# Gate steps one per unit over the experts' first products, residual products among the index picks, and another split of the weights' low parts between VectorE and GpSimd

## The chip, the cores and the metric

The program runs on one core of a Trainium2 chip. The metric is the device time of one execution in microseconds; the time of a kernel is the median over its runs.

## What is computed

The reference is two transformer blocks on 256 tokens of width 1024. The change lies in the second block's feed-forward part, which picks experts for each token:

```
q = (xc @ w_query).reshape(T, 8, 2, 128)
s1, s2 = q[:, :, 0] . sub_keys_1, q[:, :, 1] . sub_keys_2      # 128 scores per head and half
v1, i1 = top_k(s1, 16); v2, i2 = top_k(s2, 16)                 # first choice
cand   = v1[..., :, None] + v2[..., None, :]                   # 256 candidates
best, pos = top_k(cand, 16)                                    # second choice
idx = take_along_axis(i1 * 128 + i2, pos); g = softmax(best)
act = gelu(xc . expert_u[idx]); out = sum(g * act * expert_v[idx])
x = rms_norm(x + out, final_norm_g)
```

## The kernel before

Nothing is gathered: all 16384 experts are computed densely, and a gate matrix, zero where a token did not choose an expert, weights them. An expert is a pair (i, j) of sub-key numbers; one weight tile of 128 experts (one j, all i) is a unit, so there are 128 units of first products (`eu`) and 128 of second products (`ev`). They run in two halves of 64: stage A (first products of units 0 to 63, with choice and gates woven in), its second products, stage B (first products of 64 to 127, with their gates), its second products.

Products in full fp32 precision are made of fp32r halves. Each weight tile of 512 KB is loaded by SP into `raw`; ScalarE (ACT) copies it into `hi`, and VectorE (DVE) or GpSimd (POOL) makes `lo` = `raw` - `hi`; a letter per tile (`v` or `g` in `BY2` for the block's weights, `BYU` for `eu`) says which. TensorE (PE) then makes 24 products per unit, 16 with `hi` and the last 8 with `lo`. Tiles are fetched two units ahead (`ahead`), with three buffers each of `raw`, `hi` and `lo`.

Every engine works its queue in the order of the program's text, which is made by `weave`: after unit i of the first products (`experts_u`), `counts[i]` steps of a side generator are written. The lists are `CA` for stage A and `CB` for stage B. The side of stage A is `gen_a`:

- `second()`: eight steps with two heads of the second choice (`top16`, DVE alone), one that takes the positions apart, one softmax step, four index picks (one per token half t and key half i: a one-hot compare `eq`, a product with `ixr`, a tree of sums into `sel`, all on DVE), and two that transpose `sel` on PE and write `IT`, `JT`, `GHL`: 16 steps.
- `gates3()`: 33 steps, each for 8 tokens. A step makes the one-hots `oi`, `eqj` and `jg` of its tokens on DVE, and then PE makes the 16 products (line 1784) of the step before it, which ACT copies into the gates `Gt`. The last step only has products.

Stage B's side, `gen_b`, is the 33 gate steps alone. Behind its steps each generator calls `prep(0)`, which makes the first tiles of the second products: `act` times `Gt` on DVE (line 1811), `eh` on ACT, `el` on DVE. The gelu of the last two units is written when `experts_u` ends.

Ahead of stage A lies the query stage: 16 tiles of `w_query`, two per head, and the first choice of each head (`first`, `top16`) on DVE, which lags behind PE. `acc`, the four PSUM banks of the output, begins with the residual: 16 products of `xT` with the identity (line 1803; fp32, so 32 in the trace), written between the query stage and stage A.

In `CA` before, the second choice lies after units 14 to 21, positions and softmax after 24 and 25, the picks after 26, 28, 30 and 32, the transposes after 34 and 35; the gate steps run from unit 36 to 63, one per unit, but two after units 40, 45, 50, 55 and 60. In `CB` there is a gate step after every second unit from 2 to 58 and after each from 59 to 62; the entry at 63 writes `prep(0)`.

Of the kernel before, what the change touches and what calls it, by code (L numbers as in the profile page):

```python
# [13 lines left out]
AF = mybir.ActivationFunctionType  # L14
# [81 lines left out]
OUTS = (4, 6, 5, 7, 2, 3, 0, 1)  # L96
JOBS = ('hf', 'gq', 'hq', 'gk', 'gv', 'lqk', 'v5', 'v2', 'sm', 'hg', 'lg', 'z', 'fq', 'fk')
LAG = (1, 1)
CA = [0] * 14 + [1] * 8 + [0, 0, 1, 1] + [1, 0] * 4 + [1, 1] + [1, 1, 1, 1, 2] * 6
BYU = "g" * 26 + "v" * 38 + "g" * 64  # L100
CB = [0] * 2 + [1, 0] * 28 + [1] * 6

ND1 = 8
WARM = 8
# [2 lines left out]
BY1 = "v" * 37  # L107
TURNS1 = '0000000030000003030300030030010001333103030030303003300300303043004304555400510341011401000414141041000414124010142010412412420120121020112002122002002020000000000'
TURNS2 = '00000000000000000010000000100000101011011020010000100100110011212012021000202010020000020000020022022000002002020000000000000200000200000000000'
BY2 = 'vgvvvvvvgvgggvvgvgvvvvvggggvgggggggggvggvvgvvvgvgggvgvvvvgvggvvvgvg'  # L110
FU = "v"
FD = "v"

# [3 lines left out]
def _emit(ctx, tc, I, out):  # L117
    nc = tc.nc
    ctx.enter_context(tc.manual_schedule())
    V, S, G, PE = nc.vector, nc.scalar, nc.gpsimd, nc.tensor  # L120
# [20 lines left out]
    def A(o, i, f, **kw):  # L141
        t = tables.get(f)
        if t and t != table[0]:
            S.preload_act_table_set(t)
            table[0] = t
        S.activation(o, i, f, **kw)  # L146
# [6 lines left out]
    def plan(*items, by="v"):  # L153
        order.extend((n, i, w, by) for n, i, w in items)
# [40 lines left out]
    ident, mask = kept[:, 0:128], kept[:, 128:384]  # L195
    xT = keep.tile([128, 8, 256], F32)
# [13 lines left out]
    one_t = keep.tile([128, 1], F32)  # L210
# [247 lines left out]
    for lo_, hi_ in ((0, JA), (JA, 128)):  # L458
        for i in range(lo_, hi_):
            plan(("eu", i, 1024), by=BYU[i])  # L460
        plan(*[("ev", i, 1024) for i in range(lo_, hi_)])
# [769 lines left out]
    with tc.tile_pool(name="ffn", bufs=2) as fp:  # L1231
# [29 lines left out]
        acc = [bank() for _ in range(4)]  # L1261
# [399 lines left out]
    def second():  # L1661
        best = ktmp.tile([128, 2, 8, 16], F32, tag="best", name="best", bufs=1)
        pos = ktmp.tile([128, 2, 8, 16], U32, tag="pos", name="pos", bufs=1)
        for t in range(2):
            cd = ktmp.tile([128, 8, 112], F32, tag="cd", name="cd", bufs=1)
            v1, v2 = kv[:, t, 0], kv[:, t, 1]
            V.tensor_tensor(cd[:, :, 0:64].rearrange("p h (a b) -> p h a b", a=4),
                            v1[:, :, 0:4, None].to_broadcast([128, 8, 4, 16]),
                            v2[:, :, None, :].to_broadcast([128, 8, 4, 16]), op=OP.add)
            V.tensor_tensor(cd[:, :, 64:112].rearrange("p h (a b) -> p h a b", a=12),  # L1670
                            v1[:, :, 4:16, None].to_broadcast([128, 8, 12, 4]),
                            v2[:, :, None, 0:4].to_broadcast([128, 8, 12, 4]), op=OP.add)
            for h in range(0, 8, 2):
                top16(112, *((cd[:, i], best[:, t, i], pos[:, t, i]) for i in (h, h + 1)))
                yield

        ab = ktmp.tile([128, 4, 256], U32, tag="ab", name="ab", bufs=1)
        pf_ = pos.rearrange("p t h k -> p (t h k)")
        ge = ktmp.tile([128, 256], U32, tag="ge", name="ge", bufs=1)
        V.tensor_scalar(ab[:, 0], pf_, 4, None, op0=OP.logical_shift_right)  # L1680
        V.tensor_scalar(ab[:, 1], pf_, 15, None, op0=OP.bitwise_and)
        V.tensor_scalar(ab[:, 2], pf_, 2, None, op0=OP.logical_shift_right)
        V.tensor_scalar(ab[:, 3], pf_, 3, None, op0=OP.bitwise_and)
        V.tensor_scalar(ge, pf_, 6, None, op0=OP.logical_shift_right)
        abf = ktmp.tile([128, 4, 256], F32, tag="abf", name="abf", bufs=1)
        V.tensor_copy(abf, ab)
        V.tensor_scalar(abf[:, 2], abf[:, 2], 12.0, None, op0=OP.subtract)
        for i in range(2):
            V.copy_predicated(abf[:, i], ge, abf[:, 2 + i])
        abh = ktmp.tile([128, 2, 2, 8, 16], F16, tag="abh", name="abh", bufs=1)  # L1690
        V.tensor_copy(abh.rearrange("p i t h k -> p i (t h k)"), abf[:, 0:2])
        yield

        sel = ktmp.tile([128, 3, 2, 128], F32, tag="sel", name="sel", bufs=1)
        gg = sel[:, 2].rearrange("p t (h k) -> p (t h) k", h=8)
        bb = best.rearrange("p t h k -> p (t h) k")
        V.tensor_tensor(gg, bb, bb[:, :, 0:1].to_broadcast([128, 16, 16]), op=OP.subtract)
        A(gg, gg, AF.Exp)
        sm_ = ktmp.tile([128, 16], F32, tag="smk", name="smk", bufs=1)
        V.tensor_reduce(out=sm_, in_=gg, op=OP.add, axis=AX.X)  # L1700
        V.reciprocal(sm_, sm_)
        V.tensor_tensor(gg, gg, sm_[:, :, None].to_broadcast([128, 16, 16]), op=OP.mult)
        yield
        for t in range(2):
            for i in range(2):
                ixr = ktmp.tile([128, 8, 16, 16], F16, tag="ixr", name="ixr", bufs=2)
                A(ixr, kix[:, t, i, :, :, None].to_broadcast([128, 8, 16, 16]), AF.Copy)
                eq = ktmp.tile([128, 8, 16, 16], F16, tag="eq", name="eq", bufs=2)
                V.tensor_tensor(eq, abh[:, i, t, :, None, :].to_broadcast([128, 8, 16, 16]),
                                io16[:, None].to_broadcast([128, 8, 16, 16]), op=OP.is_equal)  # L1710
                V.tensor_mul(eq, eq, ixr)
                for w in (8, 4, 2):
                    V.tensor_add(eq[:, :, 0:w], eq[:, :, 0:w], eq[:, :, w:2 * w])
                V.tensor_add(sel[:, i, t].rearrange("p (h k) -> p h k", h=8), eq[:, :, 0], eq[:, :, 1])
                yield
        for t in range(2):
            p = bank("g")
            for i in range(3):
                PE.transpose(p[:, i * 128:i * 128 + 128], sel[:, i, t], ident)
            ts = slice(t * 128, t * 128 + 128)  # L1720
            two = lambda z: z[:, :, None].to_broadcast([128, 128, 2])
            V.tensor_copy(IT[:, ts], two(p[:, 0:128]))
            V.tensor_copy(JT[:, ts], two(p[:, 128:256]))
            gs = ktmp.tile([128, 128], F32, tag="gs", name="gs", bufs=1)
            V.tensor_scalar(gs, p[:, 256:384], 4096.0, None, op0=OP.mult)
            V.tensor_copy(GHL[:, ts, 0], two(gs))
            V.tensor_sub(GHL[:, ts, 1], two(gs), GHL[:, ts, 0])
            yield
# [69 lines left out]
        prep(0)  # L1798

    acc = [bank() for _ in range(4)]  # L1800
    for t in range(2):
        for k in range(8):
            PE.matmul(acc[2 * t + k // 4][:, (k % 4) * 128:(k % 4) * 128 + 128], xT[:, k, t * 128:t * 128 + 128], ident,
                      start=k % 4 == 0, stop=False, skip_group_check=True)

    W = {}
# [9 lines left out]

    def experts_v(j0, nj, last):
        for j in range(0, nj, 2):
            if j + 2 < nj:
                prep(j + 2)  # L1820
            eh, el = W.pop(j)

            def rows(i, t, v, ns=(0, 1)):
                ts = slice(t * 128, t * 128 + 128)
                for n in ns:
                    o = acc[2 * t + n]
                    n_ = slice(n * 512, n * 512 + 512)
                    PE.matmul(o, eh[:, i, ts], v[0][:, n_], start=False, stop=False, skip_group_check=True)  # L1828
                    PE.matmul(o, el[:, i, ts], v[0][:, n_], start=False, stop=False, skip_group_check=True)  # L1829
                    PE.matmul(o, eh[:, i, ts], v[1][:, n_], start=False, stop=last and j + i == nj - 1,  # L1830
                              skip_group_check=True)

            if last and j + 2 == nj:
                vs = [weight("ev", j0 + j + i) for i in range(2)]
                for t in range(2):
                    for n in range(2):
                        for i in range(2):
                            rows(i, t, vs[i], (n,))
            else:
                for i in range(2):  # L1840
                    v = weight("ev", j0 + j + i)
                    for t in range(2):
                        rows(i, t, v)
                    ahead()
            yield

    weave(experts_u(0, JA), gen_a(), CA)
    run(experts_v(0, JA, False))
    weave(experts_u(JA, 128 - JA), gen_b(), CB)
    fg = xT[:, 0:4].rearrange("p a b -> p (a b)")  # L1850
    nc.sync.dma_start(fg, I["fng"].broadcast_to([128, 1024]))
    A(one_t, one_t, AF.Ln)
    run(experts_v(JA, 128 - JA, True))


    wx.close()
    last = ctx.enter_context(tc.tile_pool(name="last", bufs=2))
# [153 lines left out]
```

## Time and profile before

| | us |
|---|---|
| time before, median of 3 runs | 1512.96 (1509.63 to 1517.84) |
| the profiled execution's own time | 1508.16 |
| its span in the trace | 1506.4 |
| PE busy in the span | 1433.6 |
| DVE, ACT, POOL busy | 995.0, 779.8, 307.6 |

Busy times add the lengths of instructions of an engine, overlaps once; a weight load of PE lies beside its products. A wait is the idle time of an engine ahead of an instruction, put down to the engine that released it. Times in rows are microseconds from the start of the span.

### The profile page before, as it was taken

Reading aid. Unit: us, or ns where it says so; the run is one execution under the profiler, and the core shown is the slowest. Engines: PE = TensorE matmul, PEld = TensorE weight load, DVE = VectorE, ACT = ScalarE, POOL = GpSimd, SP = SyncE. Lnnn points to the kernel's source line nnn. Section 1 sums busy time; section 2 is a strip of 40 time slices with the busy share of each in tenths; the row PEclk is TensorE's granted clock in tenths of the full one; section 3 lists DMA queues with packets and bytes.
Section 4 is the critical chain, followed back from the end, with each engine's and each line's share of the span. In section 5 each row is a group of like instructions: output and inputs, shape, how many; then the busy total and the mean of one; then the engine's idle time right before and its main releaser. Section 6 shows DMA issues by size and latency. Waiting matters only on the chain.

```text
span 1506.4 us, 27187 instructions
## 1 busy us (share of the span) xinstructions
PE 1433.6 (95%) x11076; PEld 1308.2 (87%) x11076; DVE 995.0 (66%) x1839; ACT 779.8 (52%) x1068; POOL 307.6 (20%) x140
## 2 busy tenths in 40 slices
PE   8699989999999899998999999999999999999998
PEld 7688858999998788898999988788889999978886
DVE  5577857997786645578937988666672333566665
ACT  5633434665563456445446566444445555554444
POOL 0000000000002125332681000000037777700000
PEclk9899969999999999999999999999999999999999
DMA  6322103566554223354554544566665555556664
GB/s 232 113 85 85 57 15 118 181 197 190 188 166 157 84 85 127 125 183 135 159 184 154 168 141 137 163 192 194 196 187 170 168 171 170 178 175 194 194 191 134
DMA packets 63791, 231.42 MB, mean 154 GB/s; under 512 B 7073, under 2 KB 7602, under 8 KB 63282
## 3 DMA queue, kind: packets, MB, share of 16 engines
q1 hardware_dynamic: 62640, 226.00, 47.5%
q10 hardware_dynamic: 1026, 3.68, 0.7%
q8 instruction: 87, 1.43, 0.4%
q14 instruction: 38, 0.31, 0.1%
HBM read 228.60 MB, written 1.05 MB: 152 GB/s over the span
## 4 chain that ended last, share of the span: by engine, by line
PE 79%; DVE 14%; ACT 4%; issue 2%; DMA 0%; DVEq 0%; SPq 0%; ACTq 0%
PE bd L314 32%; PE bm L1829 8%; PE bm L1830 8%; PE bm L1828 8%; PE bm L348 5%; PE bn L314 5%; DVE lo L164 3%; PE bn L1784 2%; ACT hi L146 1%; PE bacc L364 1%; PE bd L376 1%; PE bm L1543 1%; PE bn L933 1%; PE bn L1059 1%; PE bm L1556 1%
## 5 line engine op out<-in xcount | busy, mean ns | idle before, releaser
L146 ACT ACTIVATE hi<-raw 128x1024 fp32r<-128x1024 f32 x426 | 448.7, 1057 | 202.2 <-PE bm L1829 49.5
L164 DVE TENSOR_TENSOR lo<-raw,hi 128x1024 fp32r<-128x1024 f32 x303 | 372.2, 1234 | 173.8 <-ACT hi L146 173.8
L164 POOL TENSOR_TENSOR lo<-raw,hi 128x1024 fp32r<-128x1024 f32 x123 | 299.0, 2445 | 848.4 <-ACT hi L146 539.9
L314 PE MATMUL bd<-Xh,hi 128*128 128x256 f32 x1560 | 392.3, 289 | 9.5 <-ACT hi L146 7.3
L314 PE MATMUL bd<-Xl,hi 128*128 128x256 f32 x1560 | 382.2, 283 | 0.0
L314 PEld LDWEIGHTS bd<-Xh,hi 128*128 128x128 f32 x1560 | 296.6, 190 | 14.6 <-ACT hi L146 10.4
L314 PEld LDWEIGHTS bd<-Xl,hi 128*128 128x128 f32 x1560 | 297.1, 190 | 0.8 <-issue 0.2
L314 PE MATMUL bd<-Xh,lo 128*128 128x256 f32 x1560 | 217.3, 282 | 1.3 <-DVE lo L164 1.3
L1828 PE MATMUL bm<-hi,eh 128*128 128x512 f32 x512 | 200.5, 392 | 4.2 <-ACT eh L146 4.2
L1829 PE MATMUL bm<-hi,el 128*128 128x512 f32 x512 | 200.7, 392 | 0.4 <-DVE el L184 0.4
L314 PEld LDWEIGHTS bd<-Xh,lo 128*128 128x128 f32 x1560 | 199.3, 189 | 1.9 <-DVE lo L164 1.9
L1830 PE MATMUL bm<-lo,eh 128*128 128x512 f32 x512 | 200.4, 391 | 0.0
L1769 DVE TENSOR_TENSOR oi<-iorow,IT 128x1024 f16<-128x1024 f16 x64 | 58.6, 915 | 122.0 <-PE bn L1784 119.9
L146 ACT ACTIVATE Gt<-bn 128x512 f32<-128x512 f32 x64 | 70.9, 1108 | 116.9 <-PE bn L1784 116.9
L1828 PEld LDWEIGHTS bm<-hi,eh 128*128 128x128 f32 x512 | 96.8, 189 | 24.8 <-ACT eh L146 4.5
L1829 PEld LDWEIGHTS bm<-hi,el 128*128 128x128 f32 x512 | 96.8, 189 | 21.3 <-DVE el L184 1.1
L1830 PEld LDWEIGHTS bm<-lo,eh 128*128 128x128 f32 x512 | 96.9, 189 | 20.0
L146 ACT ACTIVATE eh<-act 128x512 fp32r<-128x512 f32 x64 | 40.4, 632 | 121.1 <-DVE act L1811 118.9
L184 DVE TENSOR_TENSOR el<-act,eh 128x512 fp32r<-128x512 f32 x64 | 44.3, 692 | 49.1 <-ACT eh L146 49.1
L1771 DVE TENSOR_TENSOR jg<-eqj,GHL 128x1024 f16<-128x1024 f16 x64 | 50.7, 792 | 2.2
L1784 PE MATMUL bn<-jg,oi 128*128 128x64 f16 x1024 | 41.0, 194 | 9.1 <-DVE jg L1771 9.1
L314 PE MATMUL bn<-Xl,hi 128*128 128x256 f32 x192 | 47.7, 286 | 0.6 <-DVE Xl L251 0.6
(588 smaller groups left out, 2062.3 us busy)
## 6 DMA issues: line engine op xcount, KB each, us to landing
raw<-in_eu SPq DMA_DIRECT2D x128, 512.0 KB, 3.5
raw<-in_ev SPq DMA_DIRECT2D x128, 512.0 KB, 3.7
raw<-in_w_in SPq DMA_DIRECT2D x61, 512.0 KB, 3.7
raw<-in_w_up SPq DMA_DIRECT2D x44, 512.0 KB, 3.6
raw<-in_w_down SPq DMA_DIRECT2D x22, 512.0 KB, 4.3
raw<-in_w_out SPq DMA_DIRECT2D x16, 512.0 KB, 3.5
raw<-in_w_query SPq DMA_DIRECT2D x16, 512.0 KB, 3.7
raw<-in_w_ba SPq DMA_DIRECT2D x4, 512.0 KB, 3.6
```

Source lines behind the costliest of these rows:

```text
L146: S.activation(o, i, f, **kw)
L164: (V if by == "v" else G).tensor_tensor(lo[:, :width], raw[:, :width], hi[:, :width].bitcast(F32), op=OP.subtract)
L184: V.tensor_tensor(lo, src, hi.bitcast(F32), op=OP.subtract)
L314: PE.matmul(o, w[:, k * 128:k * 128 + M], x[:, k], start=n == 0, stop=n == 23)
L348: PE.matmul(acc[n // 2][:, (n % 2) * 256:(n % 2) * 256 + 256], w[:, n * 128:n * 128 + 128], x, start=first and n % 2 == 0 and w is ws[0][0 ...
L364: PE.matmul(acc[n // 2][:, (n % 2) * 256:(n % 2) * 256 + 256], w[:, i * 512 + n * 128:i * 512 + n * 128 + 128], x, start=first and n % 2 = ...
L1769: V.tensor_tensor(oi, along(64), pairs(IT[:, ts], 64), op=OP.is_equal)
L1771: V.tensor_tensor(jg.rearrange("p (t i) j e -> p t i (j e)", i=2), eq.rearrange("p t j e -> p t (j e)")[:, :, None].to_broadcast([128, 8, ...
L1784: PE.matmul(p[:, t, :nj], oi[:, t].rearrange("p a b -> p (a b)"), jg[:, 2 * t + i].rearrange("p a b -> p (a b)"), start=i == 0, stop=i == 1)
L1828: PE.matmul(o, eh[:, i, ts], v[0][:, n_], start=False, stop=False, skip_group_check=True)
L1829: PE.matmul(o, el[:, i, ts], v[0][:, n_], start=False, stop=False, skip_group_check=True)
L1830: PE.matmul(o, eh[:, i, ts], v[1][:, n_], start=False, stop=last and j + i == nj - 1, skip_group_check=True)
```

## The change

The lists are written anew, the residual becomes a function that is called with each index pick, and the load of ACT's table for `Ln` moves from the front of the last second products into them.

```diff
-CA = [0] * 14 + [1] * 8 + [0, 0, 1, 1] + [1, 0] * 4 + [1, 1] + [1, 1, 1, 1, 2] * 6
-BYU = "g" * 26 + "v" * 38 + "g" * 64
-CB = [0] * 2 + [1, 0] * 28 + [1] * 6
+CA = [0] * 4 + [1] * 9 + [0] * 3 + [1, 1] + [0, 0, 1] * 3 + [0] + [1] * 35
+BYU = "g" * 18 + "v" * 46 + "g" * 64
+CB = [0] * 2 + [1, 0] * 26 + [1] * 7
...
-BY2 = 'vgvvvvvvgvgggvvgvgvvvvvggggvgggggggggvggvvgvvvgvgggvgvvvvgvggvvvgvg'
+BY2 = 'vgvvvvvvgvgggvvgvgvvvvvggggvgggggggggvggvvgvvvgvgggvvvvvvvvgggggvgg'
...
                 for w in (8, 4, 2):
                     V.tensor_add(eq[:, :, 0:w], eq[:, :, 0:w], eq[:, :, w:2 * w])
                 V.tensor_add(sel[:, i, t].rearrange("p (h k) -> p h k", h=8), eq[:, :, 0], eq[:, :, 1])
+                residual(t, i)
                 yield
         for t in range(2):
             p = bank("g")
...
         prep(0)
 
     acc = [bank() for _ in range(4)]
-    for t in range(2):
-        for k in range(8):
-            PE.matmul(acc[2 * t + k // 4][:, (k % 4) * 128:(k % 4) * 128 + 128], xT[:, k, t * 128:t * 128 + 128], ident,
+
+    def residual(t, n):
+        for k in range(4 * n, 4 * n + 4):
+            PE.matmul(acc[2 * t + n][:, (k % 4) * 128:(k % 4) * 128 + 128], xT[:, k, t * 128:t * 128 + 128], ident,
                       start=k % 4 == 0, stop=False, skip_group_check=True)
 
     W = {}
...
 
     def experts_v(j0, nj, last):
         for j in range(0, nj, 2):
+            if last and j == 4:
+                A(one_t, one_t, AF.Ln)
             if j + 2 < nj:
                 prep(j + 2)
             eh, el = W.pop(j)
...
     weave(experts_u(JA, 128 - JA), gen_b(), CB)
     fg = xT[:, 0:4].rearrange("p a b -> p (a b)")
     nc.sync.dma_start(fg, I["fng"].broadcast_to([128, 1024]))
-    A(one_t, one_t, AF.Ln)
     run(experts_v(JA, 128 - JA, True))
 
 
```

By the new `CA` the second choice lies after units 4 to 11, positions after 12, softmax after 16, the picks after 17, 20, 23 and 26, the transposes after 28 and 29, and the 33 gate steps after units 30 to 62, one each; after 63 there is none. `eu`'s low parts go to DVE from unit 18 on (26 before). By the new `CB` the gate steps lie after every second unit from 2 to 52 and after each from 54 to 60; units 61 to 63 have none, and `prep(0)` is written behind the stage's last gelu. In `BY2` the last 16 letters are the `w_query` tiles': the low parts of tiles 1, 6 and 13 go from POOL to DVE, and those of tiles 10, 11, 12 and 14 from DVE to POOL.

First place: DVE in stage A around the first double gate step (after unit 40). Before, where `lo` is a unit's low part and `oi`, `eqj`, `jg` are one step's one-hots:

```order
L164 TENSOR_TENSOR lo<-raw,hi 128x1024
L1769 TENSOR_TENSOR oi<-iorow,IT 128x1024
L1770 TENSOR_TENSOR eqj<-iorow,JT 128x512
L1771 TENSOR_TENSOR jg<-eqj,GHL 128x1024
L1769 TENSOR_TENSOR oi<-iorow,IT 128x1024
L1770 TENSOR_TENSOR eqj<-iorow,JT 128x512
L1771 TENSOR_TENSOR jg<-eqj,GHL 128x1024
L164 TENSOR_TENSOR lo<-raw,hi 128x1024
```

The same steps of the change:

```order
L164 TENSOR_TENSOR lo<-raw,hi 128x1024
L1770 TENSOR_TENSOR oi<-iorow,IT 128x1024
L1771 TENSOR_TENSOR eqj<-iorow,JT 128x512
L1772 TENSOR_TENSOR jg<-eqj,GHL 128x1024
L164 TENSOR_TENSOR lo<-raw,hi 128x1024
L1770 TENSOR_TENSOR oi<-iorow,IT 128x1024
L1771 TENSOR_TENSOR eqj<-iorow,JT 128x512
L1772 TENSOR_TENSOR jg<-eqj,GHL 128x1024
```

No two steps' one-hots stand side by side any more; a unit's low part is between them.

Second place: DVE in the query stage, between the first choices (`kv`, `kix`) of the second and third head; `lo` are tiles 10 and 11:

```order
 L1605 MAX_INDEX kix<-kv,scr 128x8 x2
 L1642 SCALAR_TENSOR_TENSOR xn<-xT,prm,R 128x256 x2
-L164 TENSOR_TENSOR lo<-raw,hi 128x1024 x2
 L184 TENSOR_TENSOR Xl<-xn,Xh 128x512
 L1597 MAX kv<-sc 128x8 x2
```

The two low parts have left DVE's queue; they stand in POOL's.

Third place: ACT at the end of stage B, from the gates' copies (`Gt`) to the first tiles of the second products (`eh`); `act` from `bd` is a gelu. Before:

```order
L146 ACTIVATE act_7924<-bd 128x512
L146 ACTIVATE Gt<-bn 128x8x64
L146 ACTIVATE hi<-raw 128x1024
L146 ACTIVATE eh<-act_7923 128x512
L146 ACTIVATE act_7924<-bd 128x512
L144 ACT_TABLE_LOAD
L146 ACTIVATE one_t<-one_t 128x1
L146 ACTIVATE eh<-act_7923 128x512
```

The change:

```order
L146 ACTIVATE Gt<-bn 128x8x64
L146 ACTIVATE hi<-raw 128x1024 x2
L146 ACTIVATE act_7908<-bd 128x512
L146 ACTIVATE hi<-raw 128x1024
L146 ACTIVATE act_7908<-bd 128x512
L146 ACTIVATE eh<-act_7907 128x512 x2
```

The last `Gt` stands two units earlier, and the first `eh` now stands behind the last gelu, which waits for PE's last first product; the table load has left this place.

## Rows read from the trace of the kernel before

**Rows 1.** Page: its span, and each engine's busy time, share of the span and instructions.

```profile
span 1506.4 us, 27187 instructions
...
PE 1433.6 (95%) x11076; PEld 1308.2 (87%) x11076; DVE 995.0 (66%) x1839; ACT 779.8 (52%) x1068; POOL 307.6 (20%) x140
```

**Rows 2.** Chain that ended last, in order of time: start, length (us), engine, tile, count.

```profile
730.62 82.37 PE bd L314 x696
```

**Rows 3.** PE's waits, 843 to 945 us: total, times, longest (us).

```profile
PE bn L1784 <- DVE jg L1771: 7.9, 5, 1.6
```

**Rows 4.** PE's timeline, 868 to 875 us: start, length, [idle before and releaser].

```profile
868.43 0.64 PE L1784 MATMUL bn<-jg,oi 128*128 128x64 f16 x16
...
871.83 0.64 PE L1784 MATMUL bn<-jg,oi 128*128 128x64 f16 x16
874.07 0.64 PE L1784 MATMUL bn<-jg,oi 128*128 128x64 f16 x16 [1.60 <-DVE jg L1771]
```

**Rows 5.** DVE's timeline around one double gate step.

```profile
928.80 1.23 DVE L164 TENSOR_TENSOR lo<-raw,hi 128x1024 fp32r<-128x1024 f32 x1 [0.51 <-ACT hi L146]
929.95 0.69 DVE L1769 TENSOR_TENSOR oi<-iorow,IT 128x1024 f16<-128x1024 f16 x1
...
931.61 0.68 DVE L1769 TENSOR_TENSOR oi<-iorow,IT 128x1024 f16<-128x1024 f16 x1
```

**Rows 6.** PE's waits, 813 to 843 us.

```profile
PE bd L314 <- DVE lo L164: 1.3, 3, 0.6
PE bn L1784 <- DVE jg L1771: 1.2, 1, 1.2
```

**Rows 7.** DVE's timeline over one index pick.

```profile
821.90 1.22 DVE L1709 TENSOR_TENSOR eq<-abh,io 128x2048 f16<-128x2048 f16 x1
...
826.20 2.35 DVE L164 TENSOR_TENSOR lo<-raw,hi 128x1024 fp32r<-128x1024 f32 x2
```

**Rows 8.** PE's timeline in the query stage, the two late lo halves.

```profile
703.79 1.21 PE L314 MATMUL bn<-xq,lo 128*128 128x256 f32 x8 [0.76 <-DVE lo L164]
...
712.97 1.80 PE L314 MATMUL bd<-xq,lo 128*128 128x256 f32 x8 [2.27 <-DVE lo L164]
```

**Rows 9.** POOL's timeline in the query stage.

```profile
708.71 2.39 POOL L164 TENSOR_TENSOR lo<-raw,hi 128x1024 fp32r<-128x1024 f32 x1 [13.64 <-ACT hi L146]
```

**Rows 10.** Stretches: length, busy PE, PEld, DVE, ACT, POOL, granted clock, DMA, GB/s.

```profile
713.00:716.00 3.00, 3.00 (x15) 3.00 (x16) 3.00 (x19) 1.45 (x2) 0.35 (x1) 0.55 0.77 240
...
730.00:765.00 35.00, 35.00 (x298) 35.00 (x297) 34.93 (x187) 16.61 (x20) 28.86 (x13) 1.00 0.54 166
945.20:948.40 3.20, 3.01 (x7) 2.18 (x8) 2.25 (x4) 1.58 (x2) 0.00 (x0) 0.53 0.07 28
1324.10:1327.30 3.20, 3.20 (x10) 2.47 (x9) 1.85 (x2) 1.99 (x4) 0.00 (x0) 0.53 0.08 32
```

**Rows 11.** Instructions of line 1803, the residual products: duration min/median/max (ns).

```profile
L1803 PE MATMUL bm<-kept,xT x32: 275/275/275, 726.9 to 730.3; 128*128 128x128 f32 x32
```

**Rows 12.** PE's timeline where each stage of second products begins.

```profile
945.09 0.54 PE L1828 MATMUL bm<-hi,eh 128*128 128x512 f32 x1 [2.50 <-ACT eh L146]
...
1322.70 0.50 PE L1828 MATMUL bm<-hi,eh 128*128 128x512 f32 x1 [1.65 <-ACT eh L146]
```

**Rows 13.** ACT's timeline at the end of the second first-products stage.

```profile
1322.02 0.63 ACT L146 ACTIVATE eh<-act 128x512 fp32r<-128x512 f32 x1 [1.89 <-DVE act L1811]
1322.55 0.58 ACT L146 ACTIVATE act<-bd 128x512 f32<-128x512 f32 x1
1323.14 1.28 ACT L144 ACT_TABLE_LOAD   x1
```

**Rows 14.** DVE's timeline, a gate step beside a POOL split.

```profile
1311.38 2.05 DVE L1769 TENSOR_TENSOR oi<-iorow,IT 128x1024 f16<-128x1024 f16 x1 [0.75 <-PE bn L1784]
...
1313.80 2.77 DVE L1771 TENSOR_TENSOR jg<-eqj,GHL 128x1024 f16<-128x1024 f16 x1
```

**Rows 15.** POOL's timeline at the same place.

```profile
1313.43 2.59 POOL L164 TENSOR_TENSOR lo<-raw,hi 128x1024 fp32r<-128x1024 f32 x1 [0.55 <-ACT hi L146]
```
## The prediction, as it went on record

> **What bounds the kernel now.** I began with the page: PE is busy for 1433.6 of 1506.4 us [rows 1], so a change can gain only what PE idles, or loses to its clock, in the stretches that it touches. DVE, at 66%, matters where PE waits for it. The chain of waits shows what PE does when nothing is late: 696 first products in 82.37 us [rows 2], which is 29 units of 24, so 2.84 us a unit. That stretch is the first 29 units of stage A, in which POOL makes the low parts and DVE is still at the choices. From there to the end of stage A I read PE's waits. Three kinds stand there. Five double gate steps cost 7.9 us [rows 3]. Around the index picks PE waits 1.3 us for `lo` and then 1.2 us for the first `jg` [rows 6]. Where the second products begin, it waits 2.50 us in stage A and 1.65 us in stage B for `eh` [rows 12]. Ahead of stage A, the query stage has two waits for `lo`, 0.76 and 2.27 us [rows 8], and the second is followed by a stretch with the clock granted at 0.55 [rows 10]. Together these are the room of the change, some 19 us; all else on PE must be executed in either order.
>
> **The change, part by part.**
>
> *Gate steps.* Single steps of stage A stand 3.40 us apart on PE (868.43 to 871.83), one unit and 16 small products, and PE waits for nothing. The second step of a double comes only 2.24 us later, after a wait of 1.60 [rows 4]. Why, DVE's rows tell: the second step's products need the `jg` that the first step's text put in DVE's queue right behind a unit's low part, 1.66 us of work a step (929.95 to 931.61) after 1.15 for `lo` (928.80 to 929.95) [rows 5]. A single step leaves a whole unit between making and using. With one step a unit DVE has 1.66 + 1.15 = 2.8 us of work against PE's 3.40, so it keeps ahead, as it does between the doubles now. All five waits should go: 7.9 us. The steps themselves, their products and their copies stay 33.
>
> *Index picks.* A pick takes DVE 4.30 us (821.90 to 826.20) and two low parts 2.35 [rows 7], so 6.65 us a pick where PE's two units take 5.7. DVE therefore falls behind, and the 1.3 and the 1.2 us follow. With three units between picks it is 4.30 + 3 x 1.18 = 7.8 us against 3 x 2.84 = 8.5, or 9.4 with the residual. Low parts are also made two units ahead, 5.7 us, which is longer than a pick. Both waits should go: 2.5 us. The eight low parts that move from POOL to DVE (units 18 to 25) fall where DVE has finished its choices: those fill the 35 us in which it is busy for 34.93 [rows 10], the first 12 units of the stage, so 18 is late enough.
>
> *The residual.* 32 products, 726.9 to 730.3 us [rows 11]: 3.6 us of PE before stage A, and 3.6 us in four pieces between units after. PE waits for nothing on either side, so I count nothing. Its cover for POOL is gone, though: stage A's first units start 3.6 us sooner against their low parts. POOL needs 2.39 us for one [rows 9] against 2.84 of a unit, so a late start is paid once and then made good; I put it at zero, at worst 1 us.
>
> *Query stage.* Tiles 10, 11, 12 and 14 leave DVE, where their low parts stand behind a first choice. The two waits, 3.0 us, should go, and the slow clock that follows the second with them: (1 - 0.55) x 3.00 = 1.35 us [rows 10]. Against this, tile 1's low part now stands ahead of DVE's additions into `xT`, which PE's next statistics need; I charge its full 1.2 us, half of the two in [rows 7]. Tiles 6 and 13 come where DVE is not late. Sum: 3.0 + 1.35 - 1.2 = 3.2 us.
>
> *The two turns into second products.* In stage A the gates now end a unit earlier, in stage B two. What is left between PE's last first product and the first second product is written the same in both: the last gelu, then `eh`, then PE. A gelu-sized step takes 0.53 us on ACT (1322.02 to 1322.55), and `eh` 0.68 from its start to PE's (1322.02 to 1322.70) [rows 12, 13], so about 1.25 us with the hand-over. In stage B `eh` now stands *ahead* of the gelu but waits for DVE's `act` product; the change puts it behind the gelu and still comes out shorter. Gains: 2.50 - 1.25 = 1.25 and 1.65 - 1.25 = 0.4 us; the wait for `el` behind it stays. The moved table load, 1.28 us [rows 13], hides in ACT's slack on either side: nothing.
>
> *End of stage B.* The seven single steps run beside POOL's low parts, where now there are five. There DVE's one-hots stretch: a `jg` that takes 0.69 elsewhere takes 2.77 and an `oi` 2.05, the first ending about when POOL's `lo` does [rows 14, 15]. PE waits for none of them now, so I count nothing; at worst see the rivals. The Trainium skill, in "SBUF — State Buffer", section "Who interferes with whom", says that a DVE instruction with two inputs in SBUF and a GpSimd one that reads SBUF shut each other out for a whole instruction. The trace agrees for this `jg`. By that rule alone each of the four low parts moved to POOL could also hold DVE up in the query stage, 4 x 2.39 = 9.6 us of DVE's time, and the sum below would shrink by as much of it as reaches PE.
>
> **Sum.** 7.9 + 2.5 + 3.2 + 1.65 = 15.2 us. The profiled execution took 1508.16 us (span 1506.4 and 1.8 around it), so 1493 for one like it. The median of the runs shown is 1512.96, 4.8 above it; on that scale it is 1497.7, and I say 1498.
>
> **Rivals.**
>
> *The clock gives more.* Each turn into second products is followed by 3.20 us at a granted 0.53 [rows 10], the lower of the clock's two levels. If shorter waits leave the clock up, each turn gains (1 - 0.53) x 3.20 = 1.5 us more: 1495. For it: 1.60 us at the doubles was not followed by a fall [rows 4], 1.65 was. Against it: the remaining 1.25 and the wait for `el` add up to nearly the same idle time.
>
> *DVE and POOL hold each other.* At the end of stage B a step and a unit need 1.66 + 2.39 = 4.05 us in turn where PE's pace is 3.40; over six sets of one-hots that is 3.9 us. If half of each moved low part in the query stage (4 x 1.2 = 4.8 us) reaches PE as well, 8.7 us are lost: 1506.5. For it speak the stretched `jg` and `oi`; against it, that PE waits for neither now, and that POOL is busy for 28.86 of 35 us beside the second choice while PE never waits [rows 10].
>
> *The waits only change their name.* If the late `jg` and `lo` come from weight tiles that land late, and not from DVE's queue, then stage A keeps its 10.4 us and the time is 1508. Against it: the single steps between the doubles wait for nothing [rows 4].
>
> *Slower.* DVE's queue is in order, and from unit 18 the low parts stand behind the picks on it, where POOL made eight of them beside it. If a low part is not made two units ahead but only when its unit is due, PE stops at each pick for the pick and its low part, 4.30 + 1.18 = 5.5 us, four times 22 us, and stage A's 10.4 stay: 1498 + 10.4 + 22 = 1530. It decides where the lead falls under 5.5 us, against 5.7 for two units. DVE's 7.8 us of work in 9.4 speak against it.
>
> **How the numbers follow.** A change of under 0.5%, 7.6 us, can hardly be told from none here. Chances: my forecast, 1494 to 1502, 0.58; the clock's extra, 0.23; DVE against POOL, 0.10, of which half lies on either side of 0.5%; the waits renamed, 0.06; slower, 0.03. So faster 0.86, same 0.11, slower 0.03. The range reaches down past the clock's rival to 1490, and up to 1505, which leaves out the upper part of DVE against POOL and all behind it.
>
> **What would show it.** In the changed kernel's trace: no wait of PE for `jg` in stage A and none for `lo` at the picks; gate products 3.40 us apart throughout; no waits for `lo` in the query stage and the clock up behind it; a wait of about 1.25 us for `eh` at both turns. I am wrong if PE waits for `lo` in the first five units of stage A, where the residual's cover is gone, if waits for `jg` appear in stage B's last steps, or if the half-speed stretches move to new places.

## The result, and the profile after

The changed kernel takes 1492.99 us (median of six runs, 1489.39 to 1493.81) against 1513.64 for the kernel before (six runs, 1509.63 to 1517.84): a ratio of 0.9863, with a 95% interval of 0.9846 to 0.9879, or 20.65 us less. The forecast was 1498, with a range of 1490 to 1505 and a gain of 15.2.

The page of the changed kernel, span and busy times, against [rows 1]:

```profile
span 1490.5 us, 27184 instructions
...
PE 1430.4 (96%) x11076; PEld 1305.4 (88%) x11076; DVE 1011.9 (68%) x1846; ACT 778.6 (52%) x1068; POOL 293.3 (20%) x133
```

The span is 15.9 us shorter, PE is busy for only 3.2 less: mostly idle time has gone. DVE has seven instructions more and POOL seven fewer, by the new split of the low parts.

PE's waits in the changed kernel around the start of the query stage (655 to 690 us), and from there to nearly the end of the program (690 to 1480); total, times, longest:

```profile
PE bm L292 <- DVE R L239: 2.1, 1, 2.1
PE bm L278 <- DVE nsq L266: 0.7, 1, 0.7
...
PE bm L1832 <- ACT eh L146: 2.9, 2, 1.6
PE bm L1833 <- DVE el L184: 0.5, 2, 0.2
```

The rows for `jg` of [rows 3, 6] and for `lo` of [rows 6, 8] are gone. The first two waits stand in the kernel before as well. What is left behind them is at the two turns. Stretches of the changed kernel (columns as in rows 10): all of stage A, the two turns, and one place in the query stage:

```profile
727.00:930.00 203.00, 203.00 (x2080) 201.64 (x2079) 178.80 (x412) 123.56 (x137) 39.96 (x18) 1.00 0.54 167
932.00:942.00 10.00, 9.11 (x39) 7.35 (x40) 6.96 (x8) 5.38 (x7) 0.00 (x0) 1.00 0.52 153
1308.00:1318.00 10.00, 9.29 (x40) 7.47 (x41) 6.95 (x8) 5.35 (x7) 0.00 (x0) 1.00 0.44 148
682.00:688.00 6.00, 4.61 (x27) 4.64 (x28) 2.51 (x7) 2.14 (x4) 0.00 (x0) 0.72 0.38 135
```

PE works for all of the 203 us of stage A. Neither turn is followed by a slow clock in this execution, where before both were [rows 10]; a slow stretch lies now at 683 us, behind the 2.1 us wait for `R`, where the kernel before had none.

PE's timeline of the changed kernel, two gate steps (against [rows 4]) and the two turns (against [rows 12]):

```profile
822.06 0.64 PE L1785 MATMUL bn<-jg,oi 128*128 128x64 f16 x16
825.46 0.64 PE L1785 MATMUL bn<-jg,oi 128*128 128x64 f16 x16
...
932.66 0.50 PE L1832 MATMUL bm<-hi,eh 128*128 128x512 f32 x1 [1.65 <-ACT eh L146]
933.39 0.51 PE L1833 MATMUL bm<-hi,el 128*128 128x512 f32 x1 [0.23 <-DVE el L184]
...
1308.47 0.49 PE L1832 MATMUL bm<-hi,eh 128*128 128x512 f32 x1 [1.21 <-ACT eh L146]
```

To see where the time came from I cut six traces at the same instructions of PE: at the first product with `w_query`, at the start of the last product with `keys`, at the first and the last second product of `hi` with `eh` in the first half, and at the first of the second half. The front, ahead of the first cut, has only one edit in it, at its very end: tile 1's low part, which DVE now makes at 664.9 us.

| us | front | query stage | stage A and turn | its second products | stage B and turn | rest |
|---|---|---|---|---|---|---|
| before | 664.1 | 62.6 | 218.3 | 175.4 | 202.2 | 183.7 |
| after | 667.4 | 59.4 | 205.9 | 174.0 | 201.8 | 182.1 |
| after, again (e1) | 669.9 | 57.9 | 205.9 | 175.6 | 201.8 | 182.0 |
| doubles (e5) | 668.3 | 59.4 | 213.4 | 175.3 | 201.8 | 182.0 |
| old letters for `eu` (e10) | 667.5 | 59.4 | 212.0 | 175.6 | 201.8 | 182.0 |
| `prep(0)` first (e11) | 667.5 | 59.4 | 204.3 | 173.4 | 200.4 | 181.5 |

From the first cut on, the changed kernel gains 3.3 + 12.4 + 1.4 + 0.4 + 1.6 = 19.1 us (19.2 before rounding). Its front took 3.3 longer in this execution, and that is not the change's: the product that lies at 624.6 us before lies at 627.8 after, 3.2 later already.

### The profile page after: what moved, and what is told of

The parts are those of the page before. It is cut to its first block, busy times and chain, and to the rows that moved or that the text cites. A ratio compares the mean times of both kernels' runs of the same rounds, so it can differ in the third digit from the quotient of the medians.

```text
span 1490.5 us, 27184 instructions
## 1 busy us (share of the span) xinstructions
PE 1430.4 (96%) x11076; PEld 1305.4 (88%) x11076; DVE 1011.9 (68%) x1846; ACT 778.6 (52%) x1068; POOL 293.3 (20%) x133
## 4 chain that ended last, share of the span: by engine, by line
PE 85%; DVE 8%; ACT 4%; issue 2%; DMA 0%; SPq 0%; DVEq 0%; ACTq 0%
PE bd L314 36%; PE bm L1833 8%; PE bm L1834 8%; PE bm L1832 8%; PE bn L314 6%; PE bm L348 5%; PE bn L1785 2%; DVE lo L164 2%; PE bacc L364 1%; PE bd L376 1%; ACT hi L146 1%; PE bn L933 1%; PE bm L1543 1%; PE bn L1059 1%; PE bm L1556 1%
## 5 line engine op out<-in xcount | busy, mean ns | idle before, releaser
L164 DVE TENSOR_TENSOR lo<-raw,hi 128x1024 fp32r<-128x1024 f32 x310 | 381.1, 1235 | 144.8 <-ACT hi L146 144.8
L164 POOL TENSOR_TENSOR lo<-raw,hi 128x1024 fp32r<-128x1024 f32 x116 | 284.0, 2464 | 846.6 <-ACT hi L146 557.0
L1770 DVE TENSOR_TENSOR oi<-iorow,IT 128x1024 f16<-128x1024 f16 x64 | 59.4, 929 | 114.3 <-PE bn L1785 112.3
L314 PE MATMUL bn<-Xh,hi 128*128 128x256 f32 x192 | 47.1, 282 | 0.0
```

Source lines behind the costliest of these rows:

```text
L164: (V if by == "v" else G).tensor_tensor(lo[:, :width], raw[:, :width], hi[:, :width].bitcast(F32), op=OP.subtract)
L314: PE.matmul(o, w[:, k * 128:k * 128 + M], x[:, k], start=n == 0, stop=n == 23)
L1770: V.tensor_tensor(oi, along(64), pairs(IT[:, ts], 64), op=OP.is_equal)
```

## Experiments

Each kernel was compared with the kernel before in runs on the same chip. The theory is the prediction's: PE's waits go because DVE and ACT have the parts ready earlier, each term by the edit named for it. The rivals: that the clock pays, or another edit than the one named.

**e1: the changed kernel again, five rounds.** No edit.

> The changed kernel once more, beside the others of this group. Order theory (PE's waits were made by the order of DVE's and ACT's queues, and the new order removes them): 0.986 of the time before, as measured first, with no wait for jg or lo in the query stage and stage A and about 1.2 to 1.7 us for eh at each turn into second products. Clock theory (a good part of the gain is where the slow stretches of PE's clock happen to fall): between 0.986 and 0.995, with half-speed stretches after one or both turns this time.

1494.11 us, ratio 0.9878 (0.9861 to 0.9896), 18.96 us. The turns' waits are the same two, but now a slow clock follows the first. First the stretch there, then PE's timeline:

```profile
932.00:942.00 10.00, 8.13 (x29) 6.31 (x29) 6.01 (x8) 4.26 (x6) 0.00 (x0) 0.83 0.32 112
```

```profile
933.69 0.51 PE L1832 MATMUL bm<-hi,eh 128*128 128x512 f32 x1 [1.64 <-ACT eh L146]
934.42 0.80 PE L1833 MATMUL bm<-hi,el 128*128 128x512 f32 x1 [0.22 <-DVE el L184]
```

The same program, the same 1.64 us, and 29 products in the stretch where the other execution had 39. The clock behind the turn is not part of what the change does for certain. In return this execution has no slow stretch in the query stage, which takes 57.9 us instead of 59.4.

**e2: only `CA`.** The kernel before with the new list for stage A; the split of the low parts, `CB`, the residual and the table load as before.

```diff
-CA = [0] * 14 + [1] * 8 + [0, 0, 1, 1] + [1, 0] * 4 + [1, 1] + [1, 1, 1, 1, 2] * 6
+CA = [0] * 4 + [1] * 9 + [0] * 3 + [1, 1] + [0, 0, 1] * 3 + [0] + [1] * 35
```

> The kernel before with the new list of stage A alone; letters, residual and stage B as before. Order theory: stage A's waits for jg and lo go by the list alone, 10.4 us and about 1 us at its turn, so about 0.992 of the time before, and the query stage keeps its two waits for lo of 0.8 and 2.3 us. Letters theory (the gain in stage A comes from taking low parts off POOL, which shuts DVE out): less than half of it, 0.996 or more, with waits for lo of 0.5 us and more at the picks, which now lie beside POOL's low parts up to unit 25.

1504.54 us, ratio 0.995 (0.9935 to 0.9966): 8.5 us, under half of the whole. No wait for `jg` is left, but a new one stands among the picks. The timeline around the picks, DVE's rows first, then one of POOL and one of PE; and under it the stretch that begins in PE's wait:

```profile
798.04 7.75 DVE L1713 TENSOR_TENSOR eq<-eq 128x1024 f16<-128x1024 f16 x3
...
812.90 1.48 DVE L1713 TENSOR_TENSOR eq<-eq 128x1024 f16<-128x1024 f16 x3
...
818.92 3.49 DVE L164 TENSOR_TENSOR lo<-raw,hi 128x1024 fp32r<-128x1024 f32 x3
...
793.89 16.56 POOL L164 TENSOR_TENSOR lo<-raw,hi 128x1024 fp32r<-128x1024 f32 x6 [0.31 <-ACT hi L146]
...
820.19 2.07 PE L314 MATMUL bd<-Xh,lo 128*128 128x256 f32 x8 [3.56 <-DVE lo L164]
```

```profile
818.90:825.70 6.80, 5.51 (x26) 5.51 (x27) 6.63 (x8) 1.06 (x1) 0.00 (x0) 0.52 0.61 187
```

With the old letters POOL still makes low parts until 810.4 us, and the early picks now run beside them. Three sums of a pick take 7.75 us there and 1.48 when POOL is done. DVE reaches its own first low parts at 818.9, PE waits 3.56 us, and 6.8 us at a clock of 0.52 begin in that wait. The Trainium skill, "SBUF — State Buffer", section "Who interferes with whom", says that a DVE instruction with two inputs in SBUF and a GpSimd one that reads SBUF shut each other out. The trace agrees, 7.75 against 1.48 us.

**e3: only the letters of `w_query`.** The kernel before with the new `BY2` (its diff stands ahead).

> The kernel before with the new letters of the query tiles alone. Order theory: the two waits for lo in the query stage, 3.0 us, go and stage A keeps its 10.4 us: 0.997 to 0.998 of the time before. POOL theory (four more low parts on POOL hold DVE up for 2.4 us each): the waits move to the first units of stage A, no gain, 1.000 or above.

1509.35 us, ratio 0.9973 (0.9954 to 0.9991): 3.7 us. The two waits of [rows 8] are gone, and one that the kernel before does not have has come, ahead of the residual. PE's and ACT's timeline:

```profile
730.72 1.16 PE L1803 MATMUL bm<-kept,xT 128*128 128x128 f32 x8 [1.30 <-ACT sc L146]
...
729.83 0.84 ACT L146 ACTIVATE sc<-bm,Rc 128x256 f32<-128x256 f32 x2 [3.17 <-DVE kix L1603]
```

PE now reaches the residual sooner than the bank that its last eight products need: the bank holds the last head's scores until ACT has copied them, and ACT waits for DVE's `kix`.

**e4: `prep(0)` ahead of the last unit.** The changed kernel with the transposes and gates of stage A one unit earlier, and `prep(0)` in both stages written ahead of the stage's last gelu, that of its last two units, instead of behind it.

```diff
-CA = [0] * 4 + [1] * 9 + [0] * 3 + [1, 1] + [0, 0, 1] * 3 + [0] + [1] * 35
+CA = [0] * 4 + [1] * 9 + [0] * 3 + [1, 1] + [0, 0, 1] * 3 + [1] * 35 + [1]
-CB = [0] * 2 + [1, 0] * 26 + [1] * 7
+CB = [0] * 2 + [1, 0] * 26 + [1] * 7 + [0, 1]
```

> The changed kernel with the transposes and gate steps of stage A one unit earlier and the first tiles of the second products written behind unit 62 in both stages, ahead of the last low part and of the last gelu. Order theory: the waits for eh of 1.65 and 1.21 us and for el of 0.23 us go, 3.3 us, and the clock stays up at both turns: 0.2% below the changed kernel, 0.984 of the time before. If the turns are bound by something else (the gates' last copy, ACT's other work), the waits stay over 1 us and the time is that of the changed kernel.

1483.71 us, ratio 0.9813 (0.979 to 0.9836). PE waits for nothing from 690 to 1480 us, and the clock stays up at both turns. The first `eh` needs the `act` of the half's first units, not the last gelu, so written ahead of that it is ready when PE arrives.

**e5: four doubles back.** The changed kernel with its transposes and gate steps begun five units later, double steps after units 40, 46, 52 and 58 and the last step behind unit 63, picks and letters as in the change.

```diff
-CA = [0] * 4 + [1] * 9 + [0] * 3 + [1, 1] + [0, 0, 1] * 3 + [0] + [1] * 35
+CA = [0] * 4 + [1] * 9 + [0] * 3 + [1, 1] + [0, 0, 1] * 3 + [0] + [0] * 5 + [1, 1] + [1, 1, 1, 1, 1, 2] * 5 + [1] * 3
```

> The changed kernel, its gate steps of stage A begun five units later and paired up again: double steps after units 40, 46, 52 and 58, three single ones to unit 63. Order theory: PE waits 1.6 us for jg at each of the four doubles, 6.4 us, and about 2.5 us for eh at stage A's turn, 7.3 us in all over the changed kernel: 0.992 to 0.993 of the time before. Rival (one-hots were late because the low parts before them landed late, from the index picks' backlog): with the picks three units apart nothing is late, no waits at the doubles, and 0.988.

1502.26 us, ratio 0.9924 (0.99 to 0.9948); stage A and its turn take 7.5 us longer than in the changed kernel. PE's waits, 850 to 960 us:

```profile
PE bn L1785 <- DVE jg L1772: 6.4, 4, 1.6
PE bm L1832 <- ACT eh L146: 2.5, 1, 2.5
```

Four doubles, four waits of 1.6, and with gates behind the last unit the turn is back at 2.5 (0.85 more). 6.4 + 0.85 = 7.25 of the 7.5; the rest is looked at below.

**e6: picks two units apart.** The changed kernel, picks after 17, 19, 21 and 23.

```diff
-CA = [0] * 4 + [1] * 9 + [0] * 3 + [1, 1] + [0, 0, 1] * 3 + [0] + [1] * 35
+CA = [0] * 4 + [1] * 9 + [0] * 3 + [1, 1] + [0, 1] * 3 + [0] * 4 + [1] * 35
```

> The changed kernel with its index picks after units 17, 19, 21 and 23 instead of 17, 20, 23 and 26, all else in place. If the spacing of two units alone made PE wait, about 1.3 us of waits for lo come back at the picks (no wait for jg, since the transposes and gate steps stay where they are): 0.989. If the waits needed the residual's absence or POOL's low parts beside the picks, none comes back, as the residual's pieces now lengthen PE's two units to 6.6 us against DVE's 6.65.

1492.91 us, ratio 0.9868 (0.9825 to 0.9912), and no wait for `lo` at the picks. The wider spacing is not what took the waits of [rows 6] away, or not it alone.

**e7: gates one unit later.** The changed kernel, transposes after 29 and 30, gate steps after 31 to 63.

```diff
-CA = [0] * 4 + [1] * 9 + [0] * 3 + [1, 1] + [0, 0, 1] * 3 + [0] + [1] * 35
+CA = [0] * 4 + [1] * 9 + [0] * 3 + [1, 1] + [0, 0, 1] * 3 + [0] * 2 + [1] * 35
```

> The changed kernel with stage A's gate steps one unit later, after units 31 to 63. Order theory: PE's wait for eh at stage A's turn grows from 1.65 to 2.5 us, nothing else moves, under 0.1% of the time. Clock theory in its turn form (the slow stretch after a turn hangs on how long PE waited there): the half-speed stretch is back after stage A's turn, 1.5 us more, and not after stage B's.

1495.12 us, ratio 0.9878 (0.9835 to 0.9921). The first turn waits as before the change, and the clock stays up all the same. PE's timeline, and the stretch around it:

```profile
938.76 0.51 PE L1832 MATMUL bm<-hi,eh 128*128 128x512 f32 x1 [2.50 <-ACT eh L146]
```

```profile
936.00:950.00 14.00, 11.28 (x56) 9.06 (x53) 9.12 (x12) 7.36 (x9) 0.00 (x0) 1.00 0.45 128
```

**e8: the residual in front.** The changed kernel, with the 32 products in one block ahead of stage A again.

```diff
-                residual(t, i)
                 yield
...
     acc = [bank() for _ in range(4)]
-
-    def residual(t, n):
-        for k in range(4 * n, 4 * n + 4):
-            PE.matmul(acc[2 * t + n][:, (k % 4) * 128:(k % 4) * 128 + 128], xT[:, k, t * 128:t * 128 + 128], ident,
+    for t in range(2):
+        for k in range(8):
+            PE.matmul(acc[2 * t + k // 4][:, (k % 4) * 128:(k % 4) * 128 + 128], xT[:, k, t * 128:t * 128 + 128], ident,
                       start=k % 4 == 0, stop=False, skip_group_check=True)
```

> The changed kernel with the residual's 16 products back in one block between the query stage and stage A. By the prediction's count: no difference, no wait. By what the run with the query letters alone showed: the last bank's four products wait about 1.3 us for ACT's last copies of the scores, which wait for DVE's first choices, and stage A's other waits stay away: 1.3 us more than the changed kernel, 0.989.

1493.56 us, ratio 0.9861 (0.9812 to 0.9911). PE's waits from 690 to 850 us are one row:

```profile
PE bm L1803 <- ACT sc L146: 1.3, 1, 1.3
```

It is the wait of e3 again, and stage A with its turn takes 1.5 us more (207.4). The medians, 1492.91 to 1495.12 for e6, e7 and e8, cannot tell so little apart.

**e9: e6 and e8 together.** A single run.

> The changed kernel with its picks two units apart, as in the run before with that spacing, and its residual in one block in front. If the residual's pieces are what hid the spacing of two units (PE's two units of 5.7 us become 6.6 with a piece, against DVE's 6.65), waits for lo of about 0.3 to 0.9 us come back at the last three picks, 1 to 2 us in all, beside 1.3 us of the block for the scores. If something else hides it (DVE's lead when the picks begin), no wait for lo appears.

1495.72 us. Even with no residual between the units, no wait for `lo` came at the picks; the one for `sc` is there. How narrow it is, DVE's and PE's timelines show (low parts of units 19 to 22 and 26, and the products with them):

```profile
781.26 1.22 DVE L164 TENSOR_TENSOR lo<-raw,hi 128x1024 fp32r<-128x1024 f32 x1
...
786.70 2.35 DVE L164 TENSOR_TENSOR lo<-raw,hi 128x1024 fp32r<-128x1024 f32 x2
...
793.27 2.35 DVE L164 TENSOR_TENSOR lo<-raw,hi 128x1024 fp32r<-128x1024 f32 x2
...
806.41 3.49 DVE L164 TENSOR_TENSOR lo<-raw,hi 128x1024 fp32r<-128x1024 f32 x3
...
787.97 1.11 PE L314 MATMUL bd<-Xh,lo 128*128 128x256 f32 x8
790.81 1.11 PE L314 MATMUL bd<-Xh,lo 128*128 128x256 f32 x8
...
796.49 1.11 PE L314 MATMUL bd<-Xh,lo 128*128 128x256 f32 x8
...
807.85 1.11 PE L314 MATMUL bd<-Xh,lo 128*128 128x256 f32 x8
```

Unit 19's part is ready at 782.5, 5.5 us ahead of PE (787.97); unit 20's at 787.9, 2.9 ahead; unit 22's at 794.5, 2.0; unit 26's at 807.6, 0.2. From unit 20 on each pick costs DVE about 0.9 us of lead, and the lead just lasts.

**e10: old letters for `eu`.** The changed kernel, with POOL making the low parts of units 18 to 25 again.

```diff
-BYU = "g" * 18 + "v" * 46 + "g" * 64
+BYU = "g" * 26 + "v" * 38 + "g" * 64
```

> The changed kernel with the low parts of units 18 to 25 back on POOL. Order theory as the prediction had it (eight low parts more or less on DVE do not matter, since its choices are through): no wait, 0.988 of the time before. By the run with the new list alone: the first picks lie beside POOL's low parts and stretch to three times their length, and PE waits some 3.6 us once for a low part that stands behind them: about 0.990.

1499.95 us, ratio 0.9925 (0.9898 to 0.9952): the letters are worth some 7 us here. PE's waits, 726 to 850 us, and under them the stretch from the end of the first on:

```profile
PE bd L314 <- DVE lo L164: 3.2, 1, 3.2
PE bd L314 <- ACT act L146: 0.7, 1, 0.7
```

```profile
809.90:813.30 3.40, 3.36 (x16) 3.36 (x17) 3.39 (x3) 0.00 (x0) 0.00 (x0) 0.51 0.70 192
```

3.2 + 0.7 + 0.49 x 3.40 = 5.6 of the 6.1 us by which stage A with its turn grew.

**e11: e4 again, five rounds.**

> The kernel with the first tiles of the second products ahead of the last gelu, a second time on another chip run. If its lead of 10 us over the changed kernel was made of the waits at the turns alone, it should be 3 to 5 us, 0.984 to 0.985; if the clock in the untouched front part falls differently for each kernel and always so for this one, 0.981 again.

1487.49 us, ratio 0.9844 (0.9819 to 0.987), beside 1492.91 for e12 on the same chip. PE's timeline is without a gap at the first turn: stretches around the second and the first:

```profile
1290.00:1316.00 26.00, 26.00 (x200) 23.93 (x199) 18.59 (x18) 16.65 (x20) 8.87 (x4) 1.00 0.63 199
926.00:946.00 20.00, 20.00 (x112) 17.46 (x111) 13.71 (x16) 12.12 (x15) 0.00 (x0) 1.00 0.60 184
```

By the table's last row, 1.6 us of the lead over the changed kernel lie in stage A, 1.4 in stage B and 0.6 in each column behind them, 4.2 in all; the medians say 10.4 (e4 beside e1) and 5.4 (e11 beside e12). In the profiled executions of e4 and e1, 6.9 us of the lead lie in the front (663.0 and 669.9 us), which is the same program in both. It is the fastest version, ahead of both kernels on both occasions, and by how much over the changed one is known to a few us only.

**e12: longer warm-up.** The changed kernel with `WARM = 11` for 8, to see whether the front's length hangs on it.

> The changed kernel with three more of its first products on PE, which feed nothing: they lie ahead of the first weight tile and shift what follows against the clock. If the front part's time is set by its waits alone, the same time within 1 us, 0.987, and the query stage begins at 667 to 670 us of the span as in the two profiles of the changed kernel. If the places where the clock falls decide, the front part moves by some us in either direction, and the query stage begins outside of that.

1492.91 us, ratio 0.9884 (0.9854 to 0.9914); its runs lie between 1484.68 and 1497.4, and its front took 666.9 us in the profile. Nothing moved that could be told from the spread.

## Why the prediction was right, and where it was off

The time fell inside the range and the direction was right; 20.65 us in place of 15.2 is a gain sized low, and 1493 lies nearer to the clock rival's 1495 than to the forecast's 1498. By its own steps:

**Gate steps, 7.9.** Right in mechanism, and shown: e5 put four doubles back and got four waits of 1.6 us, with the single steps 3.40 us apart beside them, and e2 and the change have none. The price was a little low. A step ahead of a wait shows its full 0.64 us, as in [rows 4], where 2.24 = 1.60 + 0.64; a step in the flow adds only 3.40 - 2.84 = 0.56. So such a stop costs 0.08 us more than its wait, 8.3 for five. A stop for a low part costs more still. In the kernel before the low-part products of units 30 to 33 start 3.35, 2.95 and 3.62 us apart (817.55 to 827.47, shown below), where 2.84 is the pace: the waits of 0.35 and 0.62 each cost 0.16 more at once, and the unit behind the first 0.11 more, 0.27 in all. With these prices stage A's account closes: the waits of [rows 3, 6, 12] come to 12.9 us where 1.65 is left, 11.2 less; stage A with its turn is 12.4 shorter; and six stops for `jg` at some 0.08 and three for `lo` at 0.27 make 1.3. The prediction had taken a wait for the whole cost of a stop.

**Index picks, 2.5.** The waits went, but the step given for it was not needed: "With three units between picks it is 4.30 + 3 x 1.18 = 7.8 us against 3 x 2.84 = 8.5". e6 and e9 have two units, lose lead at the predicted 0.9 us a pick, and wait for nothing. (No run had three units in the old order, so the spacing may have been enough too.) The rows speak for the lead with which DVE enters the picks. Timelines of DVE and PE in the kernel before, low parts of units 28 to 30 and the products of 28 and of 30 to 33:

```profile
806.50 1.22 DVE L164 TENSOR_TENSOR lo<-raw,hi 128x1024 fp32r<-128x1024 f32 x1
...
813.06 2.35 DVE L164 TENSOR_TENSOR lo<-raw,hi 128x1024 fp32r<-128x1024 f32 x2
...
811.87 1.11 PE L314 MATMUL bd<-Xh,lo 128*128 128x256 f32 x8
...
817.55 1.11 PE L314 MATMUL bd<-Xh,lo 128*128 128x256 f32 x8
820.90 1.22 PE L314 MATMUL bd<-Xh,lo 128*128 128x256 f32 x8 [0.35 <-DVE lo L164]
823.85 1.11 PE L314 MATMUL bd<-Xh,lo 128*128 128x256 f32 x8
827.47 1.22 PE L314 MATMUL bd<-Xh,lo 128*128 128x256 f32 x8 [0.62 <-DVE lo L164]
```

There unit 28 is ready at 807.7, 4.2 us ahead, where e9 has 5.5 for its last part ahead of the picks; and the first pick lasts from 807.6 to 813.1 instead of 4.3 us. A row of DVE's waits (765 to 845 us, kernel before), and under it ACT's timeline, say why:

```profile
DVE eq L1711 <- ACT ixr L146: 1.2, 1, 1.2
...
806.35 1.28 ACT L144 ACT_TABLE_LOAD   x1
807.64 0.60 ACT L146 ACTIVATE act<-bd 128x512 f32<-128x512 f32 x1
808.14 1.90 ACT L146 ACTIVATE ixr<-kix 128x2048 f16<-128x2048 uint32 x1
```

Behind the softmax ACT loads a table and makes a gelu, 1.8 us, before it makes the first pick's `ixr`. In the changed kernel, e6 and e9 the first `ixr` is written ahead of both, and no pick waits for it. The rest lies in the positions: DVE's first own low part is ready 5.95 us ahead of PE in the kernel before (unit 26) and in e9 (unit 18) alike, but the old order makes the positions behind it, the new one ahead of it. Together the two are 2.5 us of lead. With 2.5 us less, e9's last lead of 0.2 us would be 2.3 short, and the three stops for `lo` cost the kernel before 1.3 + 0.8 = 2.1. That these two together were the cause is read from the rows; no run had one of them alone. Nor did a run separate the 1.2 us for `jg` behind the picks.

**The letters of units 18 to 25, counted as harmless.** This step was wrong in kind: "18 is late enough" asked only whether DVE could take the parts, not what POOL does to the picks if it keeps them. Moving the picks forward needs POOL out of the way; without it the change makes a new wait of 3.2 to 3.6 us and a slow clock (e10, e2), some 7 us. The prediction's total was not hurt, since it compared the whole change.

**The residual, nothing.** In the changed kernel PE waits for nothing there, as said, and the cover that was feared lost was not needed. The step missed that a block in front would no longer have been free: with the query stage faster it meets late scores (1.3 us in e3 and e8). Spreading it saves that.

**Query stage, 3.2.** The sum came out at 3.3 and its parts did not. The charge of 1.2 us for tile 1's low part was too high: PE's wait for `nsq`, the sums that its next statistics need, went from 0.9 to 0.7 us, and the wait behind it, for `R`, stayed at 2.1. The clock's 1.35 came in e1 (57.9 us, 4.8 under the kernel before), but in the profile beside the first result a slow stretch stood at 683 us in place of that at 713, and took it back. A half-speed stretch in a new place is one of the signs that the prediction had named for being wrong.

**The turns, 1.65.** In stage B 1.21 us against 1.25. In stage A 1.65, 0.4 more: the step "What is left ... is written the same in both" overlooked DVE's queue. DVE's and ACT's timelines of the changed kernel at the first turn:

```profile
930.12 1.22 DVE L164 TENSOR_TENSOR lo<-raw,hi 128x1024 fp32r<-128x1024 f32 x1 [2.15 <-ACT hi L146]
931.26 0.68 DVE L1813 TENSOR_TENSOR act<-act,Gt 128x512 f32<-128x512 f32 x1
...
931.06 0.60 ACT L146 ACTIVATE act<-bd 128x512 f32<-128x512 f32 x1 [0.97 <-PE bd L314]
931.98 0.63 ACT L146 ACTIVATE eh<-act 128x512 fp32r<-128x512 f32 x1 [0.33 <-DVE act L1813]
```

The product `act` stands behind a low part of the second products, which waits for ACT's `hi`; ACT's `eh` waits 0.33 us for it after the gelu is done.

**End of stage B, nothing.** Right. At the stage's end DVE's one-hots are stretched beside POOL's low parts in five places, where before there were three (`oi` up to 2.89 us, where 1.10 is usual in this stage), and PE waits for none of them.

**The clock's rival, 3.0.** It came in the profiled pair: 1.4 us behind the first turn and 1.6 behind the second, which is most of what the forecast lacks against the 19.2 of the cut. The second turn kept its clock in all executions profiled with 1.2 us there, but also in e2 and e3 with 1.65. At the first turn it is chance as far as these runs tell: 1.65 us with a fall (e1, e9, e10) and without (the changed kernel, e2, e6, e8, e12), 2.50 us with (before, e3, e5) and without (e7). With no wait at all (e4, e11) there was none at either turn, in one execution of each. So the 3.0 us of the pair are luck in part; how far, these runs do not tell.

**What stays open.** The medians differ by 20.65 us in the first comparison and by 18.96 in e1. The front, in which nothing but one low part at its end was edited, took 663 to 673 us over the profiled executions, with slow stretches in different places, so a few us of any one comparison are not the change's. Two edits made alone and one taken back add up to about the whole: 8.5 (e2), 3.7 (e3) and 7.0 (e10 beside e12) make 19.2. Stage B's list and the table load had no run of their own; the second turn's 0.4 us is put down to the list by the order of the queues alone.

## What to carry to other kernels

When a piece of work is moved forward, ask which engine runs beside it at its new place: the early picks were worth 7 us less until POOL had been taken off the low parts there. Read a stall from the lead of the engine that is late, some units ahead of the stall, and not from its pace at the stall alone: a pace slower than PE's cost nothing for four picks that began 5.5 us ahead. And where PE stops at a turn between stages, look at what the first product behind it truly needs; writing that ahead of the stage's last steps (e4, e11) took both waits away.

## What the hardware did that was not expected

The granted clock fell behind a wait of 1.64 us in one execution and did not behind 1.65 at the same place of the same program in another, nor behind 2.50 in e7; by the table, a fall of some 3.4 us at a turn cost 1.3 to 1.6 us. Beside POOL's low parts a group of three fp16 sums on DVE took 7.75 us instead of 1.48, five times as long, while PE went on at its pace until its `lo` ran out.
